# Fourteen adaLN modulation blocks moved from TensorE to GpSimd products and VectorE row sums

## The chip, the cores and the metric

One core of a Trainium2 chip runs the whole program. The metric is device time in microseconds (us) of one execution; lower is better. The core's engines work side by side, each through a queue of its own in order: TensorE (PE; its weight loads are shown as PEld), VectorE (DVE), ScalarE (ACT), GpSimd (POOL), and SyncE (SP), which here only issues DMA transfers.

## The reference

One step of a diffusion backbone: two layers, 128 context tokens and 512 latent tokens (640 columns T) of width 1024. Each layer is a half-step SwiGLU feed-forward, a token mixer (layer 0: neighbourhood attention with 16 heads; layer 1: a bidirectional Hyena long convolution), and another half-step feed-forward. Every sublayer is modulated by a condition vector:

```python
sh1, sc1, g1, sh2, sc2, g2, sh3, sc3, g3 = jnp.split(jax.nn.silu(cond) @ mod_w_i + mod_b_i, N_MOD, axis=-1)
x = layer_norm(ALPHA * x + 0.5 * g1 * swiglu(modulate(x, sh1, sc1), ...), ...)
mix, extras = mixer(modulate(x, sh2, sc2))
x = layer_norm(ALPHA * x + g2 * mix, ...)
x = layer_norm(ALPHA * x + 0.5 * g3 * swiglu(modulate(x, sh3, sc3), ...), ...)
```

`cond` takes two values, one for the context tokens and one for the latent tokens. Per layer the modulation is two vectors of 1024 times a matrix of 1024 x 9216, and it is needed in pieces: shift and scale before a sublayer, the gate before its residual. All arithmetic is float32.

## The kernel before

Activations lie transposed, feature on the partitions (8 tiles of 128) and tokens along the free axis, cut into two chunks c of 320 columns. Matrix products run as three products of rounded float32 parts: high by high, low by high, high by low (`split`, L156, makes the parts with a ScalarE cast and a subtraction on VectorE or GpSimd).

**The modulation** of a layer is cut into 36 blocks of 256 outputs. `queue` puts them on a list `fill` in the order in which they are needed, with ("then", ...) entries that derive scale, shift or gate from finished blocks. A block can be computed in two ways.

*On TensorE* (`mod_block`, L217): two loads of 512 KB into two of the four `raw` buffers, eight float32 matrix products with the condition as the stationary operand (16 records in the trace, L226), a ScalarE copy (`msb`, L229), and as a second step two TensorE transposes (L236) with a small VectorE sum and an addition of the bias (`mod_finish`, L233). `fill_step` does one such step. It is called in the filter stage, at the eighth head pair of the attention (`mods`, NMOD = 8 steps), behind the attention (NFILL_A = 6 blocks), in the attention's last projection (NFILL_B = 2), inside Hyena (HFILL0 = 2 blocks, then one in each of six convolutions listed in HFILL, two steps each), behind Hyena (NFILL_C = 1) and in Hyena's last projection (NFILL_D = 4, as far as blocks are left).

*In lanes* (`mod_lanes`, L258): four loads of 256 KB (`mh`, a transposed copy of the weights), and for each half block `mod_products` (L243): four VectorE multiplications by `condw`, the condition repeated on all partitions, each of which sums its products (L247). A fold of four small products on TensorE (`mod_fold`, L253, eight records) ends the block. The four feed-forward sublayers run lanes, up to 12, 12, 12 and 9 blocks. `ffn_scope` loads `condw` and applies Silu to it (L492 to L497).

**The attention** (`attention`, L714) works on eight head pairs, each in five units t: four tiles of 128 latent queries and the context queries. `scores` (L835) does six or twelve products into two banks, then VectorE adds the bias and takes the maximum (L857), ScalarE takes exponentials (L861), VectorE scales; `turn` (L871) transposes on TensorE and splits; `weigh` (L894) multiplies with the values. A unit's scores are started one unit ahead (SAHEAD), its biases loaded BAHEAD = 3 units ahead into NBIAS = 6 tiles. Between these steps `some` interleaves other work for TensorE: the keys and queries of the next pair, values, and three quarters of the output projection (`wo_part`). The last quarter is `project` (L687) behind the attention: eight row tiles for chunk 0, then for chunk 1 while the normalisation of chunk 0 (`norm_steps`, L398) goes on in steps; the feed-forward follows.

Temporaries come from one pool of six buffers (`tmp`, L113), the raw weights from four. Instructions are put in order at build time by a list scheduler from the program order; on the chip each engine and SP's DMA queue follow that fixed order.

Of the kernel before, what the change touches and what calls it, by code (L numbers as in the profile page):

```python
# [12 lines left out]
F32 = mybir.dt.float32  # L13
F32R = mybir.dt.float32r
AF = mybir.ActivationFunctionType
ALU = mybir.AluOpType
AX = mybir.AxisListType
PSUM = bass.MemoryType.PSUM

P = 128  # L20
# [30 lines left out]
SFILL = (2, 5, 4, 4, 4, 4, 3, 0, 0)  # L51
NSUM_FFN = 7
NSUM_MIX = 6
NFILL_A = 6
NFILL_B = 2
FILL = (1, 1, 1, 1, 1, 1)
NSUM = 2
NL = (12, 12, 12, 9)
LOUT = (1, 1)
LLAST = 0  # L60
OPOOL = 3
NBIAS = 6
NAHEAD = 2
NQK = 2
NS = 4
NP = 2
NMOD = 8
BAHEAD = 3
SAHEAD = 1
WORK = ((1, 1), (1, 1), (1, 1), (1, 1), (1, 1), (1, 1), (1, 1), (1, 1))  # L70
NFILL_C = 1
NFILL_D = 4
HFILL0 = 2
HFILL = ((0, 1), (1, 0), (1, 1), (2, 0), (2, 1), (3, 0))
XPOOL = ((), ())
XDVE = (tuple(range(8)), (2, 5))
MPOOL = (2, 5, 7)
# [7 lines left out]
def kernel(  # L85
# [5 lines left out]
    te, act, dve, pool, sp = nc.tensor, nc.scalar, nc.vector, nc.gpsimd, nc.sync  # L91
# [21 lines left out]
    def tmp(name, cols=T, parts=P, dt=F32):  # L113
        t = tp.tile([P, UW], F32, tag="t", name=name)
        return t[:parts, :cols]
# [32 lines left out]
    at = {"raw": 0, "w": 0, "u": 0}  # L148
# [66 lines left out]
    mods = [const.tile([P, 72, 2], F32, name=f"mods{l}") for l in range(2)]  # L215
# [27 lines left out]
    def mod_products(raw, acc, t, g0):  # L243
        for z in range(2):
            junk = mm_bank("junk")[:, :256]
            for g in range(2):
                dve.scalar_tensor_tensor(junk, raw[:, 256 * g:256 * g + 256], 1.0, condw[0][:, z], ALU.mult, ALU.mult,  # L247
                                         accum_out=acc[:, g0 + g, t, z:z + 1])

    def mod_fold(l, blk, acc):  # L250
        ps = md_bank(f"mps{l}_{blk}")[:, 0:4]
        for g in range(4):
            te.matmul(ps[32 * g:32 * g + 32], fold, acc[:, g].rearrange("p t z -> p (t z)"), start=True, stop=True)  # L253
        ms = mods[l][:, 2 * blk:2 * blk + 2, :]
        dve.tensor_tensor(ms, ps.rearrange("p (t z) -> p t z", t=2),
                          modb[:, l, 2 * blk:2 * blk + 2].unsqueeze(2).broadcast_to([P, 2, 2]), ALU.add)

    def mod_lanes(n, half):  # L258
        while fill and fill[0][0] == "run":
            fill_step()  # L260
        last = None
        for _ in range(n):
            if not fill or fill[0][0] != "block" and last is None:
                break
            if fill[0][0] == "then" and last is not None:
                yield
                mod_fold(*last)
                fill_after()
                last = None
                yield  # L270
                if not fill:
                    break
            _, l, blk = fill.pop(0)
            acc = sm.tile([P, 4, 2, 2], F32, tag="modacc", name=f"macc{l}_{blk}")
            for i in range(4):
                t, g0 = i // 2, i % 2 * 2
                raw = half(f"mh{l}_{blk}_{i}")
                sp.dma_start(out=raw, in_=a["modt"][l, 2 * blk + t, :, 256 * g0:256 * g0 + 512])
                mod_products(raw, acc, t, g0)
                yield  # L280
                if i == 1 and last is not None:
                    mod_fold(*last)
                    last = None
            last = (l, blk, acc)
        if last is not None:
            yield
            mod_fold(*last)
            fill_after()
# [26 lines left out]
    fill = []  # L315
    tt = []
    condw = []

    def fill_after():
        while fill and fill[0][0] == "then":  # L320
# [2 lines left out]
    def fill_step():  # L323
        if fill:
            step = fill.pop(0)
            if step[0] == "run":
                step[1]()
            else:
                mod_block(*step[1:])
            fill_after()  # L330
# [155 lines left out]
    def ffn_scope(n):  # L486
        es = ExitStack()
        hp = es.enter_context(tc.tile_pool(name=f"hid{n}", bufs=1))
        pf = es.enter_context(tc.tile_pool(name=f"pf{n}", bufs=5, space=PSUM))
        units.extend(u for pair in ring for u in halves(pair))  # L490
        units.extend([hp.tile([P, 512], F32R, name=f"x{h}{i}_{n}") for h in ("h", "l")] for i in range(NUNIT - 6))
        cw = hp.tile([P, 2, 256], F32, name=f"condw{n}")  # L492
        for q in range(4):
            sp.dma_start(out=cw[32 * q:32 * q + 32].rearrange("p z k -> p (z k)"),
                         in_=a["condw"][q:q + 1].broadcast_to([32, 512]))
        act.activation(cw, cw, AF.Silu)
        condw.append(cw)  # L497
        tt.extend(hp.tile([P, 4, CH], F32R, name=f"t{i}_{n}") for i in range(6))
        at["u"] = 6

        def close():
            units.clear()
            tt.clear()
            condw.clear()
            at["w"] = 0

        es.callback(close)

        def fbank(name):
            return pf.tile([P, 512], F32, tag="f", name=name)[:, :CH]  # L510

        return es, hp, fbank
# [201 lines left out]
    def attention():  # L714
        st = 1
        with tc.tile_pool(name="at", bufs=1) as ap_, tc.tile_pool(name="psc", bufs=2, space=PSUM) as psc, \
# [3 lines left out]
            vl = [ap_.tile([P, 6, 256], F32R, name=f"vl{i}") for i in range(2)]  # L720
            biases = [ap_.tile([P, P + 256], F32, name=f"bias{i}") for i in range(NBIAS)]
            for b in biases:
                pool.memset(b[:, 0:P], 0.0)

            def sc_bank(name):
                return psc.tile([P, 512], F32, tag="sc", name=name)

# [98 lines left out]
            def bias_load(pr, t):  # L826
                for e in range(2):
                    b = biases[nb[0] % NBIAS]
                    nb[0] += 1
# [117 lines left out]
                    if dt % 2:  # L947
                        yield

            def mods():  # L950
                for _ in range(NMOD):
                    fill_step()
                    yield

            zeros = biases[0]

            def drain(it, n=100):
                for _ in range(n):
                    if next(it, it) is it:
                        return  # L960
# [15 lines left out]
            def work(p):  # L976
                out = []
                if p + 1 < 8:
                    out.append(keys_queries(p + 1))
                if p == 0:  # L980
                    out.append(group_values(1))
                if p in (3, 5):
                    out.append(group_values(p // 2 + 1))
                if p in (2, 4, 6):
                    out.append(wo_part(p // 2 - 1))
                if p == 7:
                    out.append(mods())
                return out

            units_ = [(p, t) for p in range(8) for t in range(5)]  # L990
# [13 lines left out]

            for i in range(BAHEAD):
                bias_ahead(i)
            for i in range(SAHEAD):
                start_unit(i)
            current = []
            for i, (p, t) in enumerate(units_):  # L1010
                if t == 0:
                    for w in current:
                        drain(w)
                    current = work(p)
                quota = WORK[p]

                def some(n):
                    while n > 0 and current:
                        if next(current[0], current) is current:
                            current.pop(0)  # L1020
                        else:
                            n -= 1

                nxt = i + SAHEAD
                if nxt < NU and units_[nxt][0] != p and units_[nxt][1] == 0:
                    while current and current[0].__name__ == "keys_queries":
                        if next(current[0], current) is current:
                            current.pop(0)
                bias_ahead(i + BAHEAD)
                start_unit(nxt)  # L1030
                some(quota[0])
                turn(p, t)
                if i > 0:
                    weigh(*units_[i - 1])
                some(quota[1])
            weigh(7, 4)
            for w in current:
                drain(w)
            at["w"] = 1
            ahead([("wo", 3, h) for h in range(2)])  # L1040
            return opairs[-2:]
# [194 lines left out]
    def hyena():  # L1236
        st = 4
        with tc.tile_pool(name="hy", bufs=1) as hy, tc.tile_pool(name="ptr", bufs=1, space=PSUM) as ptr, \
# [238 lines left out]
            def middle(v):  # L1477
# [15 lines left out]
                step(FILL[2])  # L1493
                if (v.pr, v.o) in HFILL:
                    fill_step()
# [5 lines left out]
                step(FILL[4])  # L1501
                if (v.pr, v.o) in HFILL:
                    fill_step()
# [3 lines left out]
            rescale(3)  # L1507
            run_fill(HFILL0)
            for pr in range(4):
# [37 lines left out]
    es, hp, fbank = ffn_scope(0)  # L1547
# [10 lines left out]
    opairs = attention()  # L1558
    run_fill(NFILL_A)
    es, hp, fbank = ffn_scope(1)  # L1560
    with es:
        ws = project_load("wo", 3)
        at["u"] = 6
        ahead_u(ffn_keys(0, 2))
        project(ws, opairs, 1, "wo3", fbank, NSUM_MIX, NFILL_B)
        ffn(0, 2, hp, fbank, ffn_keys(1, 0))
# [3 lines left out]
    es, hp, fbank = ffn_scope(2)  # L1570
# [159 lines left out]
```

## Time and profile before

| | |
|---|---|
| median of 3 runs (2797.3 to 2802.14) | 2800.18 us |
| profiled execution | 2797.45 us |
| its span, first to last instruction | 2795.6 us |
| mean granted TensorE clock, share of full speed | 0.986 |
| TensorE, VectorE, ScalarE, GpSimd busy | 2680.6, 2103.9, 1196.1, 1005.4 us |
| DMA | 293.45 MB, 105 GB/s over the span |

Times in the rows count from the start of the span. The attention's head pairs fill about 640 to 938 us, its last projection follows up to about 990, and the Hyena mixer with its own projection lies between 1940 and 2333 us.

### The profile page before, as it was taken

The page shows a single profiled execution, that of the slowest core. Times are in us where ns is not written, and L with a number is a line of the kernel's source. Part 1 is how long each engine was busy: PE and PEld are TensorE (multiplying, and loading weights), DVE is VectorE, ACT ScalarE, POOL GpSimd, SP SyncE. Part 2 cuts the span into 40 slices and gives each one's busy share as a digit, 9 for nine tenths or more (in the row PEclk, how much of TensorE's full clock was granted, in tenths as well). Part 3 has the DMA queues.
Part 4 walks back from the last instruction along what each step waited for, and adds up shares of the span by engine and source line. Part 5 has one row for each costly group of instructions (what it writes and reads, how often), then busy time and mean ns, then how long its engine had stood idle before and what let it go on. Part 6 is the DMA issues. An engine that isn't in the chain of part 4 may idle for free.

```text
span 2795.6 us, 51136 instructions
## 1 busy us (share of the span) xinstructions
PE 2680.6 (96%) x19404; PEld 2557.1 (91%) x19404; DVE 2103.9 (75%) x4762; ACT 1196.1 (43%) x2572; POOL 1005.4 (36%) x827
## 2 busy tenths in 40 slices
PE   7999999999999989999999999999999988999998
PEld 6898999989999779999989999998999988999997
DVE  6788888865765688888977888886777777765765
ACT  4662433444444473434346243344433336443433
POOL 4443543440000053534435354344223235443542
PEclk9999999999999999999999999999999998999999
DMA  7623333313222523243231333332423331322321
GB/s 270 244 78 115 121 99 121 106 60 94 79 78 71 174 90 125 91 129 121 91 106 50 125 121 99 121 113 74 133 84 106 102 99 35 99 76 76 98 69 54
DMA packets 111134, 293.45 MB, mean 105 GB/s; under 512 B 13823, under 2 KB 28927, under 8 KB 110760
## 3 DMA queue, kind: packets, MB, share of 16 engines
q1 hardware_dynamic: 107576, 285.80, 31.8%
q0 software_dynamic: 2304, 4.20, 0.5%
q8 instruction: 153, 2.51, 0.4%
q14 instruction: 93, 0.76, 0.1%
q10 hardware_dynamic: 1008, 0.19, 0.0%
HBM read 275.98 MB, written 14.16 MB: 104 GB/s over the span
## 4 chain that ended last, share of the span: by engine, by line
PE 64%; DVE 20%; DMA 6%; issue 4%; ACT 3%; POOL 3%; SPq 0%; DVEq 0%; ACTq 0%; POOLq 0%
PE f L527 7%; PE f L528 7%; PE f L529 7%; PE o L527 5%; PE o L528 5%; PE o L529 5%; DVE junk L247 5%; DVE wl L158 3%; DMA mh<-in_modt 3%; DVE xl L158 2%; PE hy L343 2%; PE hy L342 2%; PE hy L344 2%; POOL s L595 2%; PE qk L342 1%
## 5 line engine op out<-in xcount | busy, mean ns | idle before, releaser
L157 ACT CAST wh<-raw 128x512 fp32r<-128x512 f32 (+1 forms) x327 | 230.3, 709 | 305.9 <-PE o L528 150.8
L158 DVE TENSOR_TENSOR wl<-raw,wh 128x512 fp32r<-128x512 f32 (+1 forms) x274 | 270.5, 989 | 74.1 <-ACT wh L157 72.8
L527 PE MATMUL f<-xh,wh 128*128 128x320 f32 x956 | 298.0, 316 | 19.0 <-ACT sg L584 9.0
L528 PE MATMUL f<-xl,wh 128*128 128x320 f32 x956 | 298.6, 313 | 1.9 <-DVE xl L390 1.9
L529 PE MATMUL f<-xh,wl 128*128 128x320 f32 x956 | 296.2, 313 | 0.2 <-DVE wl L158 0.2
L247 DVE SCALAR_TENSOR_TENSOR junk<-mh,condw 128x256 f32<-128x256 f32 x576 | 267.4, 510 | 28.5 <-DMA mh<-in_modt 28.0
L527 PE MATMUL o<-hh,wh 128*128 128x320 f32 x840 | 260.9, 314 | 4.5 <-ACT hh L157 4.5
L528 PE MATMUL o<-hl,wh 128*128 128x320 f32 x840 | 259.1, 309 | 0.0
L529 PE MATMUL o<-hh,wl 128*128 128x320 f32 x840 | 258.0, 309 | 0.0
L353 DVE SCALAR_TENSOR_TENSOR x<-o,drv,x 128x320 f32<-128x320 f32 (+2 forms) x384 | 153.6, 433 | 103.9 <-PE o L529 103.5
L158 DVE TENSOR_TENSOR wl<-s,wh 128x512 fp32r<-128x512 f32 x187 | 170.0, 909 | 71.9 <-ACT wh L157 66.3
L157 ACT CAST wh<-s 128x512 fp32r<-128x512 f32 x187 | 115.8, 620 | 223.3 <-POOL s L593 68.7
L592 POOL TENSOR_TENSOR s<-raw 128x512 f32<-128x512 f32 x77 | 114.1, 1482 | 258.4 <-DVE junk L247 165.0
L527 PEld LDWEIGHTS f<-xh,wh 128*128 128x128 f32 x956 | 181.5, 191 | 24.3 <-ACT sg L584 9.8
L527 PE MATMUL f<-xh,xh 128*128 128x320 f32 x628 | 194.9, 314 | 8.9 <-DVE q L605 4.6
L594 POOL TENSOR_TENSOR s<-raw,raw 128x512 f32<-128x512 f32 x77 | 112.1, 1456 | 248.2 <-DVE wl L158 158.4
L528 PE MATMUL f<-xl,xh 128*128 128x320 f32 x628 | 195.2, 312 | 0.0
L529 PE MATMUL f<-xh,xl 128*128 128x320 f32 x628 | 193.6, 311 | 0.2 <-DVE xl L158 0.2
L528 PEld LDWEIGHTS f<-xl,wh 128*128 128x128 f32 x956 | 182.3, 191 | 3.8 <-DVE xl L390 3.5
L529 PEld LDWEIGHTS f<-xh,wl 128*128 128x128 f32 x956 | 181.6, 191 | 0.6 <-DVE wl L158 0.4
L527 PE MATMUL o<-hh,xh 128*128 128x320 f32 x568 | 177.1, 314 | 2.2 <-ACT hh L157 2.2
L527 PE MATMUL f<-t,wh 128*128 128x320 f32 x560 | 173.1, 310 | 3.2 <-DVE q L611 3.1
(492 smaller groups left out, 8861.3 us busy)
## 6 DMA issues: line engine op xcount, KB each, us to landing
raw<-in_win SPq DMA_DIRECT2D x176, 512.0 KB, 3.6
raw<-in_wout SPq DMA_DIRECT2D x88, 512.0 KB, 4.3
mh<-in_modt SPq DMA_DIRECT2D x144, 256.0 KB, 2.9
raw<-in_modw SPq DMA_DIRECT2D x62, 512.0 KB, 4.9
raw<-in_hyin SPq DMA_DIRECT2D x24, 512.0 KB, 3.8
ksb<-kspec SPq DMA_DIRECT2D x40, 256.0 KB, 2.7
kspec<-ks SPq DMA_DIRECT2D x32, 256.0 KB, 2.8
raw<-in_wqk SPq DMA_DIRECT2D x16, 512.0 KB, 3.7
```

What stands on the lines that cost most here:

```text
L157: act.copy(pair[0], src)
L158: (eng or dve).tensor_tensor(pair[1], src, pair[0], ALU.subtract)
L247: dve.scalar_tensor_tensor(junk, raw[:, 256 * g:256 * g + 256], 1.0, condw[0][:, z], ALU.mult, ALU.mult, accum_out=acc[:, g0 + g, t, z:z + 1])
L342: te.matmul(ps, wh[:, i, cols], kh(k), start=(i == 0), stop=False)
L343: te.matmul(ps, wh[:, i, cols], kl(k), start=False, stop=False)
L344: te.matmul(ps, wl[:, i, cols], kh(k), start=False, stop=(i == n - 1))
L353: dve.scalar_tensor_tensor(x[:, dt, sl], ps[:, o], drv[:, st, 2, dt, z:z + 1], x[:, dt, sl], ALU.mult, ALU.add)
L527: te.matmul(ps, wh, kh, start=(first and i == 0), stop=False, skip_group_check=True)
L528: te.matmul(ps, wh, kl, start=False, stop=False, skip_group_check=True)
L529: te.matmul(ps, wl, kh, start=False, stop=(last and i == n - 1), skip_group_check=True)
L592: pool.tensor_tensor(s1, a21, a22, ALU.add)
L594: pool.tensor_tensor(s3, a11, a21, ALU.subtract)
```

## The change

In the attention, a lane generator for fourteen blocks is driven by one or two steps at each of the 40 units. It uses a new form of the products: GpSimd multiplies a half block (two groups of 256) by one condition, adds the second half of each group to the first, and VectorE sums the remaining 128 elements of each group; then the same for the other condition, in place. The half block's load and the products lie in two buffers of the pool `tmp`. The attention loads `condw` for itself. The blocks at the eighth head pair, behind the attention and in its last projection are gone. Hyena computes three blocks in place of eight; what is left on the list, four blocks, falls to its last projection. The biases get four tiles in place of six and are loaded two units ahead in place of three.

```diff
-NFILL_A = 6
-NFILL_B = 2
+NFILL_A = 0
+NFILL_B = 0
-NBIAS = 6
+NBIAS = 4
-NMOD = 8
-BAHEAD = 3
+NLANE = 14
+BAHEAD = 2
-HFILL0 = 2
-HFILL = ((0, 1), (1, 0), (1, 1), (2, 0), (2, 1), (3, 0))
+HFILL0 = 0
+HFILL = ((0, 1), (1, 1), (2, 1))
...
+    def mod_products_wide(raw, acc, t, g0):
+        other = tmp("mprod", 512)
+        for z, dst in enumerate((other, raw)):
+            v = dst.rearrange("p (g k) -> p g k", g=2)
+            pool.tensor_tensor(v, raw.rearrange("p (g k) -> p g k", g=2),
+                               condw[0][:, z].unsqueeze(1).broadcast_to([P, 2, 256]), ALU.mult)
+            pool.tensor_tensor(v[:, :, 0:128], v[:, :, 0:128], v[:, :, 128:256], ALU.add)
+            dve.tensor_reduce(acc[:, g0:g0 + 2, t, z], v[:, :, 0:128], axis=AX.X, op=ALU.add)
...
-    def mod_lanes(n, half):
+    def mod_lanes(n, half, products=mod_products):
...
-                mod_products(raw, acc, t, g0)
+                products(raw, acc, t, g0)
...
+    def condition(pool_, n):
+        cw = pool_.tile([P, 2, 256], F32, name=f"condw{n}")
+        for q in range(4):
+            sp.dma_start(out=cw[32 * q:32 * q + 32].rearrange("p z k -> p (z k)"),
+                         in_=a["condw"][q:q + 1].broadcast_to([32, 512]))
+        act.activation(cw, cw, AF.Silu)
+        condw.append(cw)
...
+            condition(ap_, "at")
...
-                if p == 7:
-                    out.append(mods())
...
+            lanes = mod_lanes(NLANE, lambda name: tmp(name, 512), mod_products_wide)
             for i, (p, t) in enumerate(units_):
+                drain(lanes, 2 if i % 2 else 1)
...
-            for w in current:
+            for w in current + [lanes]:
                 drain(w)
+            condw.clear()
```

## Rows read from the trace of the kernel before

**Rows 1.** The page's list of busy time, share and instructions by engine.
```profile
PE 2680.6 (96%) x19404; PEld 2557.1 (91%) x19404; DVE 2103.9 (75%) x4762; ACT 1196.1 (43%) x2572; POOL 1005.4 (36%) x827
```
**Rows 2.** Busy us by head pair: stretch, length, engines (instructions), clock, DMA share, GB/s.
```profile
716.00:753.00 37.00, 36.70 (x286) 33.88 (x286) 29.86 (x98) 17.85 (x49) 0.00 (x0) 1.00 0.29 83
...
sum 298.00, PE 297.40 PEld 279.83 DVE 195.04 ACT 137.36 POOL 0.00; mean PE 37.17 PEld 34.98 DVE 24.38 ACT 17.17 POOL 0.00
```
**Rows 3.** Line 226 in 800 to 1050 us: durations in ns; idle us, times.
```profile
L226 PE MATMUL mps<-raw,conds x192: 379/379/403, 938.3 to 990.3; 128*32 128x256 f32 x192
...
  DMA raw<-in_modw: 17.4, 18
```
**Rows 4.** TensorE in order of time: start, duration, line, form, count, idle before.
```profile
938.32 1.07 PE L226 MATMUL mps<-raw,conds 128*32 128x256 f32 x16
...
944.97 0.44 PE L881 MATMUL tp<-ident,S 128*128 128x128 f32 x2
...
950.74 0.36 PE L909 MATMUL pvc<-ph,vh 128*128 128x256 f32 x1
...
955.01 0.39 PE L527 MATMUL wo<-xh,wh 128*128 128x320 f32 x1
...
972.01 0.70 PE L401 MATMUL mu<-s,mean_w 128*128 128x320 f32 x2
...
990.02 0.64 PE L226 MATMUL mps<-raw,conds 128*32 128x256 f32 x8 [4.07 <-DMA raw<-in_modw]
...
994.39 0.63 PE L527 MATMUL f<-xh,xh 128*128 128x320 f32 x1 [1.63 <-DVE xh L386]
```
**Rows 5.** The same view behind the Hyena mixer.
```profile
2304.41 1.16 PE L527 MATMUL ho<-xh,wh 128*128 128x320 f32 x5 [1.64 <-ACT xh L157]
...
2318.09 0.81 PE L401 MATMUL mu<-s,mean_w 128*128 128x320 f32 x2 [0.73 <-POOL s L357]
...
2332.91 0.63 PE L527 MATMUL f<-xh,wh 128*128 128x320 f32 x1 [1.98 <-DVE xh L386]
```
**Rows 6.** A fold on TensorE, in order of time.
```profile
1110.20 0.25 PE L253 MATMUL mps<-macc,fold 128*32 128x4 f32 x8
```
**Rows 7.** A modulation block inside Hyena, in order of time.
```profile
2100.44 1.07 PE L226 MATMUL mps<-raw,conds 128*32 128x256 f32 x16
```
**Rows 8.** GpSimd: ns min/median/max of one line, then groups (busy, mean, idle).
```profile
L592 POOL TENSOR_TENSOR s<-raw x77: 1264/1302/2986, 139.9 to 2710.6; 128x512 f32<-128x512 f32 x77
...
L593 POOL TENSOR_TENSOR s<-s,raw 128x512 f32<-128x512 f32 x77 | 116.7, 1516 | 63.3 <-POOL s L592 25.9 <-DVE junk L247 16.5 <-issue 8.3
...
L1405 POOL TENSOR_TENSOR U<-U,V 128x256 f32<-128x256 f32 x32 | 27.4, 858 | 42.8 <-DVE V L1397 36.9 <-PE iv L1434 3.1 <-DVE mods L241 1.6
```
**Rows 9.** VectorE groups by form in the attention, 640 to 920 us.
```profile
L158 DVE TENSOR_TENSOR wl<-raw,wh 128x1024 fp32r<-128x1024 f32 x24 | 29.4, 1224 | 24.3 <-ACT wh L157 24.1
L158 DVE TENSOR_TENSOR pl<-tp,ph 128x512 fp32r<-128x512 f32 x28 | 19.2, 687 | 2.7 <-ACT ph L157 2.2
...
L158 DVE TENSOR_TENSOR pl<-tp,ph 128x256 fp32r<-128x256 f32 x34 | 14.2, 418 | 2.2 <-ACT ph L157 2.1
...
L353 DVE SCALAR_TENSOR_TENSOR x<-wo,drv,x 128x320 f32<-128x320 f32 x19 | 10.4, 545 | 1.3 <-PE wo L529 1.3
```
**Rows 10.** VectorE groups by form in a feed-forward layer, 1100 to 1400 us.
```profile
L158 DVE TENSOR_TENSOR wl<-raw,wh 128x512 fp32r<-128x512 f32 x33 | 29.7, 900 | 2.7 <-ACT wh L157 2.6
...
L353 DVE SCALAR_TENSOR_TENSOR x<-o,drv,x 128x320 f32<-128x320 f32 x24 | 13.0, 543 | 2.2 <-PE o L529 2.2
```
**Rows 11.** Line 496, Silu of the condition: durations in ns; idle us, times.
```profile
L496 ACT ACTIVATE condw<-condw x3: 631/632/633, 144.5 to 2313.3; 128x512 f32<-128x512 f32 x3
L496 ACT ACT_TABLE_LOAD  x2: 1283/1283/1283, 963.0 to 2312.0; - x2
...
  DMA condw<-in_condw: 9.9, 2
```
**Rows 12.** Line 830, the bias loads: time to landing.
```profile
DMA to landing us min/median/max: 2.0/2.2/3.6
```

More of the change, by code (lines that the diff above doesn't have):

```diff
@@ L491, in ffn_scope @@
         units.extend([hp.tile([P, 512], F32R, name=f"x{h}{i}_{n}") for h in ("h", "l")] for i in range(NUNIT - 6))
[L492 to L497, printed above, removed]
+        condition(hp, n)
         tt.extend(hp.tile([P, 4, CH], F32R, name=f"t{i}_{n}") for i in range(6))
@@ L948, in wo_part @@
                         yield
[L950 to L953, printed above, removed]
             zeros = biases[0]
```

## The prediction

> **What bounds the kernel now.** I read the page's engine list first: TensorE is busy for 96% of the span, VectorE for 75%, GpSimd for 36% [rows 1]. That makes TensorE the limit on average, so a change that takes work from it can pay, but only where TensorE, and not a chain of waits, sets the time. So I went to the stages. In the attention, cut into its eight head pairs (640 to 938 us), TensorE is busy for 297.4 of 298 us, VectorE for 195.0 and GpSimd for nothing at all; VectorE's fullest pair, 716 to 753, has 29.9 of 37 us [rows 2]. Nothing but TensorE matters there, and an idle engine stands beside it. Behind it comes another picture. Twelve TensorE blocks (192 matmul records, 16 to a block) lie within 938 to 991 us, where TensorE idles 17.4 us in 18 places for their weights [rows 3]. In order of time [rows 4]: two blocks stand ahead of and between the scores and transposes of the last units; the last transposes come at 944.97, the context product at 950.74, the output projection of the last quarter at 955.01, its first mean at 972.01; at 990.02 a block ends a wait of 4.07 us; the feed-forward layer begins at 994.39. The same steps behind the Hyena mixer, with few blocks in them, are the measure of what they cost alone: projection at 2304.41, mean at 2318.09, feed-forward at 2332.91 [rows 5].
>
> **Part by part.** Before, TensorE computes 36 blocks (14 in the filter stage, 4 + 6 + 2 around the end of the attention, 10 in and behind Hyena) and the lanes of the feed-forward layers 36. After, the attention's lanes take 14, so the queue reaches Hyena with 64 blocks done in place of 62: 3 blocks inside Hyena in place of 8, one behind it as before, and 4 in place of 1 in its last projection.
>
> *The end of the attention.* The last unit's scores no longer wait behind two blocks of 1.07 us (the row at 938.32 and one like it 2 us later), its transposes not for the blocks between 942 and 945, and the context product at 950.74 not for blocks after it; I put the projection at 947 where it was at 955.0, 8 us sooner (bounds 2, the two blocks alone, and 9). The first half of the projection ran 17.0 us from 955.01 to 972.01 with eight groups of block matmuls of 0.64 us among them, 5.1 us: 11.9 without. Hyena's half took 13.7. From mean to feed-forward Hyena's chain took 14.8 us against 22.4 here, which held the wait of 4.07 [rows 4, 5]. So the feed-forward starts at 947 + 11.9 + 14.8 = 973.7 in place of 994.4: **20.7 us gained**. Bounds: 13 if the projection moves by 2 us and then takes the whole of Hyena's 28.5 us (955.0 - 2 + 28.5 = 981.5), 27 if it moves by 9 and the first half is rid of another 5 us of waits.
>
> *Folds.* A lane block needs one fold on TensorE, eight small records in 0.25 us [rows 6]. In the attention nothing hides it: 14 x 0.25 = **3.5 us lost**.
>
> *Hyena.* A block there costs 1.07 us [rows 7] plus two transposes, 0.44 us for two of the same shape at 944.97 [rows 4], together 1.4 since each begins before its forerunner ends. Five fewer are 7.0 us; two of them are the first pair, whose place is followed by waits anyway, so I count **6 us gained** (bounds 4 and 7). The three more in the last projection cost 3 x 1.4 = **4.2 us**; bounds 0, if they lie in waits of that stage, and 12, three waits like the 4.07 us; a gain is excluded, since the work is added. Each asks two loads of 512 KB through SP and two of the four raw buffers, which the next feed-forward weights need too.
>
> *GpSimd.* A half block is two products of 512 and two halving sums of 256 elements. The nearest rows are the additions of 512, at 1.26 us least, 1.30 in the median and 1.52 in the mean of the dearer line, and of 256, at 0.86 in the mean [rows 8]. A sum waits for its product; the line at L593 loses 25.9 us in 77 to such a wait, 0.34 each. At the low prices a half is 2 x (1.26 + 0.73) + 0.7 = 4.7 us (0.73 is drawn from the 512 row in proportion with 0.1 added, an estimate), at the mean prices 2 x (1.52 + 0.86) + 0.7 = 5.5. 56 halves are 263 or 308 us against 298. VectorE is what makes such additions dear in the feed-forward layers, and in the attention most of its operands come from PSUM, so I take 4.9, 274 us: hidden, with 8% to spare. Cover gone, each 0.1 us above 5.32 costs 5.6 us.
>
> *VectorE.* 112 row sums over 2 x 128 elements. The trace has no such sum; one 256-wide instruction takes 0.42 us [rows 9], bounded by half the price of a 512-wide one, 0.34, and by that of a 320-wide one, 0.545. 112 x 0.42 = 47 us (38 to 61). Besides, GpSimd slows those VectorE instructions that read two SBUF operands: a split of 512 costs 0.90 us in the feed-forward, while a residual from PSUM costs 0.543 there and 0.545 in the attention [rows 9, 10]. Only the 24 weight splits (29.4 us) are of that kind, so up to 9 us. Together 195 + 56 = 251 of 298 us: hidden on average, but 716 to 753 would want 29.9 + 7 + 1.3 = 38 of 37 us, and a row sum that comes up before its product makes all softmax work behind it wait, then the transposes. I put **4 us lost** (bounds 0 and 25).
> The Trainium skill (GPSIMD Engine Reference, Specifications) lets only VectorE instructions with two SBUF inputs, or in a two-port mode, contend with GpSimd; the trace agrees with 0.90 against 0.543. By that rule alone the row sums, with one input, would not suffer and the stall would be nothing: 4 us better than the sum below.
>
> *ScalarE and queues.* The attention now loads the condition for itself and passes it through Silu: a table load of 1.28 us and 0.63 of work, **1.9 us lost** at its start, where TensorE is not covered by the attention; the two waits for that load before sum to 9.9 us, which is the other bound [rows 11]. SP issues 56 loads of 256 KB, each held until one of six shared temporaries is free, and weights, cached keys and biases stand behind them. Biases are asked for two units ahead in place of three; a unit is 298/40 = 7.45 us and a bias lands in 2.2 [rows 12], so I count nothing; if SP is held a unit long, that cover is gone and the scores wait.
>
> **Sum:** -20.7 + 3.5 - 6 + 4.2 + 1.9 + 4 = -13.1 us. The profiled execution took 2797.45 us, so 2784.3; it lies 2.7 us below the median of the runs. I forecast **2784 us**, its own range 2768 to 2795 (the good end takes the tail and Hyena at their bounds and every other loss but the folds as nothing: -27 + 3.5 - 7 = -30.5, 2767; the bad end the tail at its other bound with 3 us of stall more: -13 + 3.5 - 6 + 4.2 + 1.9 + 7 = -2.4, 2795).
>
> **Rivals.** *The blocks only filled waits.* The softmax chain of the last pair and the first normalisation chain run as long as before, and only 2 us and the 4.07 us wait come back, with 2 us of blocks. For it: TensorE has 17.4 us of idle time there, VectorE and ScalarE hand work to and fro. Against: Hyena's 28.5 us against 39.4. Time: -8 + 3.5 - 6 + 4.2 + 1.9 + 4, nothing: **2797**.
> *VectorE waits for GpSimd.* A row sum finds its product late by one sum-to-product gap, 0.34 us, 112 times: 38 us, which makes VectorE 289 of 298 us. About half of it reaches TensorE in the pairs with output projection: +19 - 4 on the forecast, **2799**. Against: two or three halves are in flight, so the product can be early.
> *GpSimd sets the pace, slower than before.* From 5.32 us a half on, the attention lasts as long as GpSimd. At 5.9 us, 7% above the mean prices, it lasts 330 us, 32 more: **2815**. For it: the mean prices alone already give 308 us, and a half holds two of the six temporaries from its load to its last row sum. Against: the low prices hold where VectorE reads PSUM.
> The Trainium skill speaks for this rival (GPSIMD Engine Reference, Engine selection): elementwise work with two inputs belongs on VectorE, GpSimd being about twice as slow. The trace agrees on the ratio, 1.26 us for 512 elements against 0.69 on VectorE.
>
> **Chances.** The forecast 0.64, the first rival 0.14 (a third of it still faster), the second 0.10 (half same, half slower), the third 0.12. No difference a measurement of this kernel can tell is about 0.2%, 5.6 us. Faster 0.64 + 0.04 = 0.68; same 0.10 + 0.05 = 0.15; slower 0.05 + 0.12 = 0.17. The range for 8 in 10 goes from 2768 to 2806: it leaves out the third rival and a little more at either end.
>
> **What would show it.** Right: no L226 matmul between 640 and 1000 us, the first feed-forward matmul 15 to 25 us sooner, GpSimd busy 230 to 290 us inside the attention, and TensorE still above 97% in its pairs. The tail is wrong if the step from last projection to feed-forward still takes 35 us or more. The stall is wrong if VectorE's row sums show idle time before them, released by GpSimd, of more than 10 us, or if transposes and folds on TensorE wait for VectorE. Three blocks too many in Hyena's projection would show as TensorE waiting for modulation weights after 2290 us. What would sink the forecast is a half block above 5.3 us on GpSimd.

## The result and the profile after

The changed kernel takes **2849.47 us** (median of 4 runs, 2847.33 to 2858.76) beside 2798.74 for the kernel before: a ratio of 1.018, 95% interval 1.0162 to 1.0196. The forecast was 2784 us with a range to 2806; the change cost 50 us.

The page's engine list, which answers [rows 1]:
```profile
PE 2694.7 (95%) x19264; PEld 2572.0 (90%) x19264; DVE 2192.7 (77%) x4860; ACT 1193.0 (42%) x2561; POOL 1236.4 (43%) x1049
```
TensorE has 140 records fewer and is busy 14 us longer, in a span 50 us longer. It did not get slower work; it waited, and part of the time ran at a lower clock. The places come from the times at which the same products start in both traces (each span ends with its own records; FFN 1 and 2 run from chunk 1's `rs` product of one normalisation to chunk 0's of the next):

| stretch | before | after | difference |
|---|---|---|---|
| attention, first to last product of the scores | 297.4 | 338.5 | **+41.1** |
| from there to the output projection | 15.4 | 18.6 | +3.2 |
| projection to feed-forward | 39.4 | 28.1 | **-11.3** |
| FFN 1 and FFN 2 behind the attention | 437.5, 439.5 | 446.1, 447.7 | **+8.6, +8.2** |
| Hyena, up to its last projection | 362.2 | 362.7 | +0.5 |
| normalisation behind it, chunk 0 to chunk 1 | 21.3 | 24.9 | +3.6 |
| all the rest together | | | -4 |

The attention, in busy us by stretch (length, then TensorE, weight loads, VectorE, ScalarE, GpSimd; clock, DMA share, GB/s): first two strips of 40 us of the kernel before, then of the kernel after, with the whole of its scores.
```profile
640.00:680.00 40.00, 40.00 (x323) 37.97 (x323) 22.16 (x68) 18.81 (x52) 0.00 (x0) 1.00 0.24 74
720.00:760.00 40.00, 39.70 (x300) 36.58 (x298) 31.06 (x98) 17.64 (x49) 0.00 (x0) 1.00 0.28 81
```
```profile
640.00:680.00 40.00, 38.36 (x306) 35.38 (x306) 31.14 (x77) 16.92 (x49) 26.81 (x26) 1.00 0.36 112
720.00:760.00 40.00, 36.94 (x234) 32.32 (x232) 36.96 (x91) 15.06 (x41) 35.65 (x35) 0.83 0.34 103
...
641.00:979.00 338.00, 318.15 (x2395) 290.40 (x2395) 279.97 (x726) 138.44 (x383) 225.58 (x214) 0.96 0.36 110
```
The whole: TensorE idles 338 - 318 = 20 us where it idled 0.6, the clock of 0.96 is worth about 13.5 us more (4% of 338, an estimate), the folds 3.5: 37 of the 41 us. GpSimd, busy for 226 us, did not run out of time. The strip from 720 us is the pair with output projection of [rows 2]: VectorE rises to 37 of 40 us and TensorE does 234 matmuls in place of 300. Five microseconds at a time, the same view:
```profile
725.00:730.00 5.00, 5.00 (x39) 4.45 (x38) 4.47 (x14) 0.81 (x2) 3.05 (x4) 1.00 0.77 231
730.00:735.00 5.00, 4.15 (x34) 2.93 (x32) 4.12 (x7) 3.60 (x9) 4.61 (x6) 1.00 0.29 96
735.00:740.00 5.00, 3.97 (x20) 3.70 (x20) 4.89 (x15) 1.31 (x4) 5.00 (x6) 0.67 0.66 201
740.00:745.00 5.00, 5.00 (x29) 4.59 (x29) 3.84 (x9) 1.82 (x6) 5.00 (x5) 0.50 0.35 92
745.00:750.00 5.00, 4.80 (x21) 4.32 (x20) 4.87 (x14) 0.96 (x2) 3.65 (x5) 0.50 0.15 55
750.00:755.00 5.00, 5.00 (x36) 4.57 (x36) 4.79 (x16) 2.05 (x6) 5.00 (x6) 0.96 0.34 106
```
TensorE idles 0.85 and 1.03 us in two neighbouring rows, and the granted clock falls to 0.50, its 1.2 GHz level, for more than ten: a row then holds 20 to 29 matmuls in place of 39. Here a stall of 2 us is paid several times over: in the 40 us from 720 us TensorE does 66 matmuls fewer, 8.7 us at the pace of the kernel before (39.7 us for 300).

VectorE's groups by form between 640 and 940 us (busy, mean ns, idle before); they answer [rows 9], two of whose forms are here again, unchanged:
```profile
L158 DVE TENSOR_TENSOR wl<-raw,wh 128x1024 fp32r<-128x1024 f32 x24 | 37.4, 1559 | 10.3 <-ACT wh L157 10.0
L878 DVE TENSOR_SCALAR S<-S,sm 128x320 f32<-128x320 f32 x26 | 20.6, 832 | 0.2
L257 DVE TENSOR_REDUCE macc<-mprod 128x2 f32<-128x256 f32 x45 | 18.4, 410 | 7.5 <-POOL mprod L256 7.5
L158 DVE TENSOR_TENSOR pl<-tp,ph 128x512 fp32r<-128x512 f32 x27 | 18.4, 682 | 0.3
...
L873 DVE TENSOR_SCALAR sm<-sm 128x2 f32<-128x2 f32 x34 | 16.1, 473 | 0.2
...
L370 DVE SCALAR_TENSOR_TENSOR x<-wo,drv,x 128x320 f32<-128x320 f32 x16 | 8.6, 539 | 0.3 <-PE wo L541 0.2
...
L876 DVE RECIPROCAL sm<-sm 128x2 f32<-128x2 f32 x33 | 5.3, 160 | 14.5 <-ACT S L875 14.4
```
Of the kernel before, the same three softmax lines:
```profile
L864 DVE TENSOR_SCALAR S<-S,sm 128x320 f32<-128x320 f32 x32 | 10.9, 381 | 0.4
...
L862 DVE RECIPROCAL sm<-sm 128x2 f32<-128x2 f32 x39 | 6.4, 163 | 24.1 <-ACT S L861 24.0
L859 DVE TENSOR_SCALAR sm<-sm 128x2 f32<-128x2 f32 x39 | 6.3, 161 | 0.4
```
The scaling of the probabilities went from 381 to 832 ns, the negation of two numbers a partition from 161 to 473, the weight split from 1224 to 1559. What reads one operand from PSUM (682 against 687, 539 against 545) did not move at all, and neither did the reciprocal of two numbers a partition (163 and 160), which lies in SBUF as the negation does. So it is not every VectorE instruction, and not every one in SBUF. The negation and the scaling stand on the chain from scores to transposes.

TensorE in order of time at the end of the attention, answering [rows 4]:
```profile
983.49 1.79 PE L895 MATMUL tp<-ident,S 128*128 128x128 f32 x6 [2.96 <-DVE S L878]
...
992.81 0.39 PE L923 MATMUL pvc<-ph,vh 128*128 128x256 f32 x1
...
997.72 0.60 PE L539 MATMUL wo<-xh,wh 128*128 128x320 f32 x1 [4.12 <-DVE xl L158]
...
1008.95 0.70 PE L418 MATMUL mu<-s,mean_w 128*128 128x320 f32 x2
...
1025.79 0.63 PE L539 MATMUL f<-xh,xh 128*128 128x320 f32 x1 [1.96 <-DVE xh L403]
```
From projection to mean 11.2 us and on to the feed-forward 16.8: that part of the forecast held (11.9 and 14.8). The projection itself waits 4.12 us for VectorE and starts no sooner after the last scores than before.

### The profile page after: what moved, and what is told of

Read it like the earlier page. It is cut to its first block, busy times and chain, and to the rows that moved or that the text cites. A ratio compares the mean times of both kernels' runs of the same rounds, so it can differ in the third digit from the quotient of the medians.

```text
span 2845.5 us, 51261 instructions
## 1 busy us (share of the span) xinstructions
PE 2694.7 (95%) x19264; PEld 2572.0 (90%) x19264; DVE 2192.7 (77%) x4860; ACT 1193.0 (42%) x2561; POOL 1236.4 (43%) x1049
## 4 chain that ended last, share of the span: by engine, by line
PE 48%; DVE 15%; issue 3%; DMA 3%; POOL 3%; ACT 3%; DVEq 0%; ACTq 0%; POOLq 0%; SPq 0%
PE f L539 6%; PE f L540 6%; PE f L541 6%; PE o L539 5%; PE o L541 4%; PE o L540 4%; DVE wl L158 3%; DVE junk L247 3%; DMA mh<-in_modt 2%; PE hy L360 2%; PE hy L359 2%; PE hy L361 2%; DVE xl L158 1%; POOL s L607 1%; POOL s L606 1%
## 5 line engine op out<-in xcount | busy, mean ns | idle before, releaser
L158 DVE TENSOR_TENSOR wl<-raw,wh 128x512 fp32r<-128x512 f32 (+1 forms) x274 | 282.2, 1031 | 56.8 <-ACT wh L157 55.5
L539 PE MATMUL f<-xh,wh 128*128 128x320 f32 x956 | 297.8, 315 | 27.8 <-DVE q L617 16.8
```

What stands on the lines that cost most here:

```text
L158: (eng or dve).tensor_tensor(pair[1], src, pair[0], ALU.subtract)
L539: te.matmul(ps, wh, kh, start=(first and i == 0), stop=False, skip_group_check=True)
```

## The experiments

Three theories stood against each other. **A**: GpSimd's work as such slows those VectorE instructions that need what GpSimd uses. **B**: VectorE has too much to do, or its row sums stand in its queue waiting for products. **C**: the transfers, the shared temporaries or the shorter bias look-ahead. In the table, scores, idle and clock are read as above, each in its own trace; the ratio is to the kernel before on the same chip, where its median was 2800.6 to 2803.8 us.

| run | median us | ratio (95%) | scores | idle | clock | FFN 1, 2 |
|---|---|---|---|---|---|---|
| e1 no row sums | 2836.53 | 1.0107 to 1.0153 | 322.1 | 12.7 | 0.99 | 448.2, 448.2 |
| e2 no GpSimd | 2827.44 | 1.0076 to 1.0116 | 313.6 | 6.9 | 0.98 | 448.8, 452.2 |
| e3 loads and folds | 2813.94 | 1.0025 to 1.0062 | 301.6 | 0.0 | 1.00 | 445.8, 448.4 |
| e4 before, four bias tiles | 2803.23 | 0.9993 to 1.0023 | 297.4 | 0.6 | 1.00 | 436.5, 440.3 |
| e5 softmax on ScalarE | 2818.72 | 1.0048 to 1.0088 | 316.6 | 5.8 | 0.98 | 445.6, 449.2 |
| e6 the same in before | 2807.70 | 1.0002 to 1.0024 | 301.8 | 0.0 | 1.00 | 438.4, 439.7 |
| e7 twelve blocks | 2826.02 | 1.0055 to 1.0097 | 332.3 | 17.8 | 0.97 | 443.3, 440.8 |
| e8 before, shifted | 2825.47 | 1.0057 to 1.0095 | 297.3 | 0.6 | 1.00 | 447.0, 446.1 |
| e9 GpSimd alone | 2818.34 | 1.0045 to 1.0077 | 308.4 | 7.0 | 1.00 | 440.9, 441.5 |
| e10 twelve, softmax on ScalarE | 2809.19 | 1.0014 to 1.0045 | 318.9 | 8.8 | 0.98 | 438.2, 440.3 |
| e11 e10, merged row sums | 2831.12 | 1.0093 to 1.0132 | 339.1 | 19.7 | 0.95 | 440.6, 440.5 |
| e12 eight, in light pairs | 2813.88 | 1.0035 to 1.0074 | 316.6 | 6.2 | 0.99 | 437.3, 440.5 |

**The parts by themselves.** e1 is after with GpSimd's work but no row sums, e2 with row sums over the loaded weights but no GpSimd work, e3 with loads and folds and neither:
```diff
 e1 -            dve.tensor_reduce(acc[:, g0:g0 + 2, t, z], v[:, :, 0:128], axis=AX.X, op=ALU.add)
 e2 -            pool.tensor_tensor(...)   # all four of a half block
 e3 +        dve.tensor_copy(acc[:, g0:g0 + 2, t, 0], raw[:, 0:2])   # in place of both
```


> The changed kernel with its loads, GpSimd products and halving sums and folds, but without VectorE's 112 row sums; each block's accumulator is set to a constant, so the modulation of fourteen blocks is a constant. The changed kernel starts the last projection of the attention at 997.7 us against 955.0 before, 42.7 later. Theory A, GpSimd's traffic slows VectorE: without the sums VectorE still waits, the small softmax scalings of 160 ns still take 350 or more and the start of the projection stays 25 to 40 us late; the whole takes 2825 to 2845. Theory B, VectorE is overloaded by the sums and waits for their products: with 45 us of sums and their waits gone, the projection starts by 955 and the whole takes 2790 to 2800.

> The changed kernel with its loads, row sums (over halves of the loaded weights) and folds, but with no GpSimd work in the lanes; the modulation of fourteen blocks is wrong by that. Theory A, GpSimd's traffic slows VectorE: the small softmax scalings are back at 160 ns, the projection starts at 940 to 958 us and the whole takes 2780 to 2805. Theory B, the sums overload VectorE: the projection is still 20 us late or more, the whole 2815 or more.

> The changed kernel with its loads and folds, one tiny VectorE copy from each loaded half and neither products nor row sums; the modulation of fourteen blocks is a constant. Theory C, SP's queue, the shared temporaries and the shorter look-ahead of the biases cost the time: the projection still starts 20 us late or more. Theories A and B: it starts at 938 to 950, and what stays of the loss is the part behind the attention, where the feed-forward layers are 14 us longer in the changed kernel than before and Hyena's last projection 4 us; the whole takes 2770 to 2790 if these 14 us go with the attention's lanes, 2785 to 2805 if they stay.

Of the 41.1 us in the scores, loads and folds alone cost 4.2, row sums alone another 12.0, GpSimd's work alone another 20.5, and the two together 4.4 more than their sum. So A is the largest part and B a real one. In e1 the softmax lines were as slow as in the kernel after (772 and 508 ns), in e2 and e3 as fast as before (380 and 158). By its total e2 falls where B was expected, and e3 lies above both of its ranges; 24 and 17 us of these totals are in the feed-forward layers, which come below, so the parts are read from the scores alone.

Theory C's transfers fall: e3 has all the loads, and TensorE idles nowhere, though VectorE waits 25.0 us for these loads there. The temporaries are tested less: e2 and e3 hold one for each half block in place of two, and e3 frees it after one small copy. How much of e1's 20.5 us comes from temporaries that GpSimd holds was not separated.

**The bias look-ahead**, the kernel before with `NBIAS = 4` and `BAHEAD = 2`:

> The kernel before with four bias tiles in place of six, loaded two units ahead in place of three, and nothing else. Theory C: 5 us or more slower. Theories A and B: within 5 us of the kernel before.

No difference, as the prediction had it.

**GpSimd with nothing attached.** The kernel before, with products on a scratch tile that nobody waits for:
```diff
+                for _ in range(2 if i % 5 == 4 else 3):
+                    pool.tensor_tensor(scratch, scratch, scratch, ALU.mult)
+                    pool.tensor_tensor(scratch[:, 0:256], scratch[:, 0:256], ones[:, 0:256], ALU.mult)
```


> The kernel before (with four bias tiles, which changed nothing) and, in the attention, 112 GpSimd multiplications of 512 and 112 of 256 elements on a scratch tile of their own: no load, no shared temporary, no row sum, no fold, and nothing waits for them. Theory A (GpSimd's work as such holds up VectorE's all-SBUF instructions at the doubled rate and its splits): while GpSimd runs, some 240 us, the scalings take about 0.8 us in place of 0.38 and the negations about 0.5 in place of 0.16, and the scores stretch goes from 297 to 313 to 320 us; total 2816 to 2824. Theory C (loads through SP, shared temporaries, waits for products): nothing of these is here, the stretch stays at 297 to 300 and the total at 2799 to 2805.

Its strips and its scaling line (all of 640 to 940 us, of which GpSimd ran up to 845):
```profile
640.00:680.00 40.00, 40.00 (x323) 38.07 (x321) 28.36 (x69) 19.23 (x52) 37.02 (x39) 1.00 0.25 74
...
720.00:760.00 40.00, 34.94 (x252) 29.49 (x251) 36.03 (x91) 16.70 (x48) 36.94 (x40) 1.00 0.26 78
```
```profile
L868 DVE TENSOR_SCALAR S<-S,sm 128x320 f32<-128x320 f32 x30 | 20.0, 707 | 0.3
```
Work that touches nothing of the attention costs it 11.0 us, so A holds; less than the 16 us or more expected, and less than the 20.5 of e1. GpSimd also did less here: it started before the scores and was busy for 187 us of them, up to 845, against 223 us in e1, where it goes on to their end; in proportion that makes 13 us (an estimate). What costs the other 7 us in e1, where GpSimd starts and stops with the loads and holds temporaries, is open. GpSimd is busy for 37 us in both strips. Where VectorE goes from 22 to 28 us, TensorE does its 323 matmuls as before; where it goes from 31 to 36, TensorE idles for 5 us. The slowing is everywhere, the price only where VectorE was already full. The clock stayed at 1.00 in that strip, so not every stall of TensorE is followed by a lower clock; which ones are, these runs do not settle.

**Softmax off VectorE.** The negated maximum and the scalings go to ScalarE, in after (e5) and in before (e6):
```diff
-                dve.tensor_scalar(ng, mx, -1.0, None, ALU.mult)
+                act.activation(ng, mx, AF.Identity, scale=-1.0)
...
-                    dve.tensor_scalar(S[e], S[e], su[:, e:e + 1], None, ALU.mult)
+                    act.activation(S[e], S[e], AF.Identity, scale=su[:, e:e + 1])
```


> The kernel after, with two of the softmax's small VectorE instructions of each unit done by ScalarE: the negated maximum and the two scalings by 1/sum. GpSimd's products and VectorE's row sums stay. Theory A (GpSimd slows those VectorE instructions that have all operands in SBUF and run at the doubled rate: the scalings took 0.83 us in place of 0.38, the negations 0.47 in place of 0.16, and they lie on the chain from scores to transposes): most of the 20.5 us of the GpSimd part and the 4.4 us of interaction come back, the scores stretch goes from 338 to 318 to 324 us, the total to 2829 to 2836. Theory B (VectorE's load and its row sums behind the products make the loss): VectorE's load falls by about 70 us in that stretch, but the row sums still stand in its queue and still meet their products late, so 12 us or more of the loss stays and the rest comes back only in part: 328 to 334, total 2839 to 2845. Theory C (transfers and temporaries): no change, 2849.

> The kernel before with the same two softmax steps on ScalarE; the control for the run above. GpSimd is idle in that stretch, VectorE is busy for 195 of 298 us, and TensorE sets the time. Theory A: nothing to gain, 2799 to 2805; if the negation and scaling cost more on ScalarE, or ScalarE's queue holds them up, up to 6 us slower. Theory B: if VectorE's load as such were what costs time, taking about 35 us from it would make this kernel faster too, by 3 us or more.

In after it gives back 30.8 us, 21.9 of them in the scores and 7.0 between the scores and the feed-forward; in before it costs 4. So VectorE's load as such was no limit in the kernel before. In after, e5 takes away the load of these lines together with what GpSimd added to it, and does not separate the two.

**The feed-forward layers.** Nothing in them was changed, but all of e1 to e3 had lost 8 to 13 us in each. With fourteen blocks in the attention, their lanes start at block 40 of the list in place of 38. e7 gives them block 38 back (after with `NLANE = 12` and Hyena's blocks as before), e8 takes it from the kernel before (`NFILL_A = 8`, `HFILL0 = 0`):

> The kernel after with twelve blocks in the attention's lanes in place of fourteen, and Hyena's eight blocks back as before, so that the feed-forward layers and everything behind them take the same blocks as in the kernel before. Theory A, with the feed-forward's loss put down to where its lanes begin in the list of blocks (block 40 in place of 38): FFN layers back to 437 to 440 us each from 446 to 448 (16 us), the last projection 4 us shorter, the attention 338 - 41 x 2/14 = 332 us, together 2849 - 16 - 4 - 6 = 2823. Rival (the feed-forward lost for another reason, such as the bias tiles, the loads of condw or the state in which the queues are left): FFN stays at 446 to 448, total 2838 to 2842.

> The kernel before, with two of the blocks that TensorE computes inside Hyena done behind the attention instead (eight there in place of six), so that the feed-forward lanes begin at block 40, as they do after the change. No GpSimd work is added. Theory that the place in the list costs the feed-forward its 8 us: both FFN layers behind the attention go from 437.5 and 439.5 to 445 to 448 us, total 2801 + 16 + 2 (two more blocks in the tail) - 2 (two fewer in Hyena) = 2815 to 2819. Rival: the FFN layers stay at 437 to 440, total 2800 to 2803.

In the layers both are as the theory says: e8 pays 16 us with no GpSimd work (its total lies 6 us above the forecast, since the two more blocks behind the attention cost that part 10.6 us and not 2), e7 has the second layer back at 440.8 and the first at 443.3, in a profiled execution that lay 10 us above its median; e10 to e12, with the same list, have 437 to 441. TensorE's waits in FFN 1 (us, times, longest), of before, of e8 and of after:
```profile
PE f L527 <- DVE q L605: 3.5, 3, 2.4
```
```profile
PE f L527 <- DVE q L605: 8.1, 6, 3.0
```
```profile
PE f L539 <- DVE q L617: 8.1, 6, 3.2
```
Behind eight and four blocks in turn a ("then", ...) entry stands in the list, at which the last block is folded at once and scale, shift or gate derived. Two blocks further on, these places fall beside other tiles of the feed-forward, and TensorE waits longer for VectorE's `q`: 4.6 of the 9.5 us that FFN 1 loses in e8. That this is the way from list to wait is argued from the order of the code; that the place in the list costs 16 us is measured.

**Towards a better version.** e10 joins both remedies; e11 adds a third halving on GpSimd and one row sum for each half block; e12 drives eight blocks only in pairs without output projection and leaves four to TensorE at the eighth pair:
```diff
 e11 +            pool.tensor_tensor(o[:, :, 128 + 64 * z:192 + 64 * z], v[:, :, 0:64], v[:, :, 64:128], ALU.add)
 e11 +        dve.tensor_reduce(acc[:, g0:g0 + 2, t, :], o[:, :, 128:256].rearrange("p g (z k) -> p g z k", z=2), ...)
 e12 -                drain(lanes, 2 if i % 2 else 1)
 e12 +                drain(lanes, {0: 2, 1: 2, 3: 2, 5: 2, 6: 100 if t == 0 else 0}.get(p, 0))
```


> The kernel after with twelve blocks in the attention's lanes, Hyena's eight blocks back, and the negation and the scalings of the softmax on ScalarE: the two remedies found so far together. If they add: attention 316.6 less two fourteenths of its 19 us, 314 us; feed-forward layers 438 and 440 in place of 446 and 449; last projection back to before's; total 2818.7 - 17 - 4 - 3 = 2795 (2790 to 2801), no slower than the kernel before. Rival: the feed-forward's loss does not go with the place in the list when the lanes run in the attention (the twelve-block run had 443 us in the first of them): 2802 to 2808.

> The kernel of the run before with one row sum for each half block in place of two: GpSimd halves each product once more (128 to 64) into a free part of the first product's buffer, and VectorE sums 2 x 2 x 64 elements at once, 0.41 us in place of 2 x 0.41. VectorE has 48 instructions and 20 us less, and waits for GpSimd once for each half; GpSimd has 96 more of 128 elements, about 0.55 us each by proportion, so a half block takes 5.4 us and the 48 of them 260 us. Theory B's part (12 us for the row sums): half of it comes back, 5 to 7 us, total 2789. Theory A: the longer GpSimd work slows the splits that are left, 24 of 1024 elements, a little more, so the gain is 0 to 5 us; if 5.4 us a half is too slow for the attention, nothing or a loss.

> Eight lane blocks in place of twelve, driven only in the head pairs without output projection (pairs 0, 1, 3 and 5), four blocks back on TensorE at the eighth pair as in the kernel before, the softmax's negation and scalings on ScalarE, Hyena's eight blocks as before. Theory A with the loss where VectorE was already full: in the kernel before VectorE has 22 to 26 of 40 us in those pairs and 29.5 to 31 in the ones with output projection, where the kernel after loses most (234 matmuls in place of 300 between 720 and 760 us). With the heavy pairs free of GpSimd, the scores stretch is 300 to 306 us in place of 319, the tail keeps its gain of 11 us, total 2794 to 2802, at or below the kernel before. Rival (the loss goes with the number of half blocks, wherever they lie): the stretch is 297 + 21 x 8/12 + 4 = 315 us, total 2804 to 2810.

e10 is 40 us better than the kernel after and still 0.3% behind the kernel before: the feed-forward is whole again, but the scores kept 318.9 us where 314 was expected, and Hyena took 366.4 where the profile of before has 362.2 (more on this below). e11 was a plain miss, 22 us worse with 48 row sums fewer. One row of VectorE in order of time shows why, with GpSimd's rows of the same moment below it:
```profile
725.78 7.05 DVE L158 TENSOR_TENSOR wl<-raw,wh 128x1024 fp32r<-128x1024 f32 x1 [0.21 <-ACT wh L157]
732.76 0.48 DVE L812 SCALAR_TENSOR_TENSOR qk0l<-qk,qk0h 128x320 fp32r<-128x320 f32 x1
```
```profile
725.87 1.30 POOL L255 TENSOR_TENSOR mprod<-mh,condwat 128x512 f32<-128x512 f32 x1
727.12 0.74 POOL L257 TENSOR_TENSOR mh<-mh 128x256 f32<-128x256 f32 x1
...
730.59 0.47 POOL L258 TENSOR_TENSOR mprod<-mprod 128x128 f32<-128x128 f32 x1
731.01 0.74 POOL L257 TENSOR_TENSOR mh<-mh 128x256 f32<-128x256 f32 x1
```
A split that takes 1.22 us alone took 7.05. GpSimd ran one instruction behind the other until 731.75; the split ended 1.08 us later. TensorE then waited 2.4 us for `qk0l`, behind it in VectorE's queue, and the clock fell to 0.50 again. e12 came out at the rival's 315 us for the scores (316.6), but is no verdict on the light pairs: 20 half blocks in the first two pairs were more than GpSimd had time for (38.6 and 37.8 of 40 us), and the rest ran into the third, the heavy one, where 237 matmuls were done in place of 300. A slower pace there, and the splits on another engine, were not tried. No version beat the kernel before.

## Why the prediction was wrong

- **The step that failed** is "Only the 24 weight splits (29.4 us) are of that kind ... I put 4 us lost". The softmax's scalings and negations are of that kind too, with one SBUF operand each. [Rows 9] did not list them, but the trace of before held a sign: the scaling of 384 columns took 0.416 us and of 128 columns 0.280, 0.53 ns a column, where the split from PSUM takes (687 - 418) / 256 = 1.05. It is the scaling, at the doubled rate, that GpSimd slowed, and the split from PSUM that it did not. The weight splits themselves were priced rightly: 29.4 us became 37.4, where up to 9 more were forecast. Others of their kind, two SBUF operands, were left out: the splits of the cached keys, on the way to the scores, went from 284 to 834 ns. Measured: 37 us in the scores in place of 4, beside the folds; GpSimd's work alone makes 20.5 of them and the row sums alone 12.0 (e1, e2).
 The Trainium skill says it in one place (SBUF — State Buffer, Who interferes with whom): a VectorE instruction in a two-port mode, which a tensor_scalar may enter, is fully blocked by a GpSimd instruction that was issued first, and a row sum or an instruction with one SBUF input outside those modes is not. The trace agrees on each: 381 to 832, 410 ns for row sums beside GpSimd's work and 411 without it (e2), 545 to 539 for residuals. The rule that the prediction cited (the Trainium skill, GPSIMD Engine Reference, Specifications) names the two-port mode as well; which lines here run in it was not asked. That the doubled rate is this mode is inferred from the rate and the slowing; no run shows it directly. The rule speaks of one GpSimd instruction; e11's split of 7.05 us was held while eight of them ran.
 The comparison that the prediction sets beside that rule, 0.90 against 0.543, is of 512 columns and 320. At 512 columns with two SBUF operands and GpSimd idle, a split took 0.688 us (two in e3), so GpSimd added 0.21 us and not 0.36.
- **The heavy pair** was named in the prediction, "38 of 37 us", and then priced at a tenth of what it cost. VectorE, full and on the chain that feeds TensorE, cost more than its excess of 1 us: 3 us of TensorE's idle time and 0.17 of the clock, 6.8 us, in that one strip.
- **The rivals.** "VectorE waits for GpSimd" did occur: row sums waited 11.7 us in the stretch, over the 10 named as the sign, but a third of the 38 us it reckoned with. What these waits cost TensorE was not separated: in e2 the row sums cost 12.0 us with no GpSimd to wait for, and in e3 25.0 us of VectorE's waits for loads left TensorE no idle time. "GpSimd sets the pace" was wrong: a half block took 4.35 us (the means of its four instructions, 1358, 850, 1305 and 840 ns), less than the 4.9 assumed, and GpSimd stood 68 us of the scores waiting for loads. Two figures of the prediction are 1 us off their own sums (2815 for 2816 there, and a range from 2768 for 2767), which changes nothing.
- **The tail.** Mean to feed-forward and the first half of the projection came out as argued, -11.3 us of a forecast -20.7. The 8 us for the projection itself did not come: the blocks there had filled waits of the softmax chain, the first rival for that part. e3, with no GpSimd work and no row sums, also needs 17.4 us from the last scores to the projection (15.4 before). With nothing to fill the waits the clock fell as well; TensorE from the last scores on, in before and in e3:
```profile
940.00:955.00 15.00, 11.15 (x107) 6.20 (x107) 9.14 (x33) 7.96 (x24) 0.00 (x0) 1.00 0.91 323
```
```profile
947.00:965.00 18.00, 9.12 (x38) 7.43 (x37) 9.83 (x31) 9.98 (x29) 0.00 (x0) 0.57 0.24 71
```
- **The feed-forward**, +16.8 us, was in no term. The prediction counted how many blocks each layer computes and not at which block its list begins.
- **Hyena** seems to give nothing back for five blocks fewer where 6 us were forecast, but the profile of before is the exception there: the seven other traces with eight blocks take 365.4 to 367.5 us, the five with three blocks 362.1 to 364.4, so by these some 3.7 us came back, though a single trace can lie as far off (e8, with six blocks, takes 360.9). TensorE idles 15 to 18 us with eight blocks and 20 to 21 with three, so part of the blocks had filled waits. The three more in its last projection cost 3.6 us (4.2 forecast), folds and loads 4.2 (3.5 for folds), a row sum 0.41 us (0.42).

## What to carry to other kernels

Before giving work to an idle GpSimd, list by form the VectorE instructions it will run beside, and look for a slope that shows the doubled rate as well as for two SBUF operands; then price the stage where VectorE is fullest, not the mean. Price a stall of TensorE at more than its length: here 3.1 us of idle time in a strip went with a clock of 0.83, and blocks that only filled waits had kept the clock at 1.00 where it was 0.57 without them (e3); but 5.1 us of idle time in e9 left the clock as it was. A list of work that several stages draw from is shifted for all of them by a change in one.

## What the runs showed that was not expected

- GpSimd can hold a VectorE instruction for longer than one of its own: min, median and max of the 1024-wide splits are 1214, 1225 and 1227 ns before, and 1209, 1562 and 7047 in e11:
```profile
L158 DVE TENSOR_TENSOR wl<-raw,wh x24: 1209/1562/7047, 644.7 to 939.0; 128x1024 fp32r<-128x1024 f32 x24
```
 In the kernel after, with the softmax lines on VectorE, the longest of this stretch was 2352. Splits of over 5 us came only in e5 and e10 to e12, which have those lines on ScalarE. Why is open.
- Of the slowed kinds, the smaller an instruction, the more it suffers in proportion: 161 to 473 ns in the mean for the negation of two elements a partition, 1224 to 1559 for a split of 1024. It is the kind that counts and not the size: the reciprocal of two elements kept its 160.
- Hyena with the same blocks took 362.2 us at a clock of 0.99 in the profile of before and 365.4 to 367.5 at 0.97 to 0.98 in seven other traces. A difference of 4 us between two single profiles is not yet one between two kernels.
